# Three FFN-input tile pairs as dense products by token halves, and a LayerNorm end without GpSimd, in a two-layer streaming encoder kernel

## The chip, the cores and the metric

The kernel runs on one core of one Trainium2 chip, as one program of 39,733 instructions. The metric is the device time of one execution in microseconds (us). The engines are TensorE (PE, with its weight loads, PEld), VectorE (DVE), ScalarE (ACT), GpSimd (POOL) and SyncE (SP), which issues most of the DMAs.

## What is computed

Two post-norm layers on a residual stream h of 544 tokens (512 of a prompt and 32 of a sample) and 1024 channels. Each layer runs four token mixers on h, projects their gated sum, and then an FFN with a hidden width of 2816:

```python
    h = layer_norm(ALPHA * h + merged @ w_out, ln1_g, ln1_b)
    a, u = jnp.split(h @ w_ffn_in, 2, axis=-1)
    h = layer_norm(ALPHA * h + (jax.nn.silu(a) * u) @ w_ffn_out, ln2_g, ln2_b)
```

All of it is in float32. The kernel gets that precision from three products of a value's high and low part.

## The kernel before

**Layout.** Channels lie on the 128 partitions, tokens on the free axis, in two halves of 272 tokens (`HB`), called h0 and h1. A value is split into a high part (`hi`, a copy on ACT) and a low part (`lo`, a subtraction on DVE, or on POOL where a letter "g" says so). A product of two such values is three matmuls, hi by hi, lo by hi and hi by lo (`mm3` L712, `product` L737). A dense tile of 128 output channels over 1024 input channels takes 8 x 3 = 24 matmuls for each token half. Its weights are one tile of 128x1024, split as `whi` and `wlo` (`wsplit` L705).

**Order.** The code records every operation, and a planner (`schedule` L544) gives each engine its order, with modelled times; operations inside `ahead` come earlier by a number of places. `places` L179 packs the tiles into the on-chip memory. Where the plan has a gap on PE, `fillers` L626 puts small matmuls into a bank that nobody reads (`bank<-idle`, L648). All other instructions come from one line, L650, so rows are told apart by the tiles' names. Each engine then works its own queue in order.

**From the projection to the FFN.** `project_out` makes eight dense tiles of y = ALPHA*h + merged @ w_out (names `mhl`, `whi`, `wlo`, `y`); the last four for h0 and then for h1, each half followed by `ln_end`, the end of the LayerNorm. That sums over channels on PE with a matrix of ones, makes rs (the inverse deviation) and nmr (minus mean times rs), both named `lnw`, and then runs over eight tiles m: ACT makes t = g*nmr + b, DVE makes y = y*g*rs (`y<-y,gb,lnw`), POOL adds t (`y<-y,lnw`), and y is split into `h0hi`, `h0lo` or `h1hi`, `h1lo`. For h1 ahead of the FFN only odd m are split, since the FFN input needs no others; and after each odd m the differences T1 to T4 of two tiles and both halves are made (`T_plain`, then a split into two parts named `T`), two on DVE and two on POOL ("vvgg").

**FFN input.** `ffn` has 22 pairs of tiles, one of a and one of u, taken in groups of 6, 8 and 8. Each pair is a 2x2 block product in Strassen's form with 7 instead of 8 products of 12 matmuls: 84 where the dense form has 96. The operands on the token side are B11 and B21 (even and odd tiles of h0), B22 (odd tiles of h1) and T1 to T4. On the weight side they are sums of blocks, split as `wop` (128x512; `wsum`, `ws`, `wa`, `wt`, `raw` are what they are made from). B11 and B21 need only h0, so the first `EARLY` = 10 pairs have their two products with them made ahead (`corner` L745, 24 matmuls); half of these have an operand split on POOL (`CORNER`). `strassen` L775 makes the other five. `ln_end` also ends the second LayerNorm of layer 0 ("in").

Of the kernel before, what the change touches and what calls it, by code (L numbers as in the profile page):

```python
# [24 lines left out]
HB = NT // 2  # L25
# [3 lines left out]
FF = 2816  # L29
NM = D // 128  # L30
# [61 lines left out]
LONG = 300  # L92
SELECT = (2, 2, 1)
LEAD = 800
EARLY = 10
PUSH = 120
GROUPS = ((0, 6), (6, 8), (14, 8))
CORNER = ("vg", "vv") * 6
PIECES = ([(0, 512, "v"), (512, 1024, "v")], [(0, 512, "a"), (512, 768, "a"), (768, 1024, "g")], [(0, 1024, "v")])
SPLITS = ("vvvvvvv", "vvvvvvv", "vvvvvvv", "vgvgvgv")  # L100
RESIDUAL = 2
# [45 lines left out]
class Memory:  # L147
# [31 lines left out]
    def places(self, virtual):  # L179
        if self.stage == 1:  # L180
            return self.places_first()
        ops = self.plan.ops
        n, cells = len(self.size), (SBUF - sum(a * b for a, b in RINGS.values())) // self.GRAIN
        size, born, last = (np.array(x) for x in (self.size, self.born, self.last))

        true = virtual.plan.ops
        ready = np.zeros(len(ops))
        for i, op in enumerate(true):
            ready[i] = max((ops[j].done + Plan.HOP[ops[j].eng][op.eng] for j in op.after), default=-1.0)
        for i, op in enumerate(ops):  # L190
            if ready[i] < 0:
                ready[i] = min((ops[j].start for j in true[i].then), default=op.start) - (op.done - op.start) - 1.0
            ready[i] = max(ready[i], min(op.latest, op.start) - MARGIN)
        start, end = np.full(n, 1e9), np.full(n, -1e9)
        for b, users in self.users.items():
            start[b] = min(ready[i] for i in users)
            end[b] = max(ops[i].done for i in users)
        at, done = np.zeros(n, dtype=np.int64), np.zeros(n, dtype=bool)
        life = last - born
        todo = np.flatnonzero(size > 0)  # L200
        self.late = 0.0
        for b in sorted(todo, key=lambda b: (life[b] < 4000, -size[b] * life[b] if life[b] > LONG else b)):
            early = born[b] > last
            late = last[b] < born

            over = np.where(early, end - start[b], np.where(late, end[b] - start, 1e9))
            cost = np.full(cells, -SPARE)
            for x in np.flatnonzero(done & (over > -SPARE)):
                c = cost[at[x]:at[x] + size[x]]
                np.maximum(c, over[x], out=c)  # L210
            top = np.lib.stride_tricks.sliding_window_view(cost, size[b]).max(1)
            k = int(top.argmin())
            if top[k] >= 1e9:
                raise MemoryError((b, size[b], born[b], last[b]))
            at[b], done[b] = k, True
            self.late += max(0, top[k])
        return at
# [438 lines left out]
class Build:  # L656
# [175 lines left out]
            self.split(out(n, 0), out(n, 1), out(n, 1).plain)  # L832

    def hx(self, part, k, h):
        return self.H[h][part][:, k, :]

    def new_h(self, h):
        self.H = list(self.H)
        self.H[h] = [self.mem.tile([128, NM, HB], F32R, name=f"h{h}{n}") for n in ("hi", "lo")]

    def first_load(self, l):
# [922 lines left out]
    def ln_end(self, ln, h, to, scale=1.0):  # L1764
        nc = self.nc
        p1, p2 = self.tps("p1"), self.tps("p2")
        mean, msq, var, rs, nmr = (self.stat(ln, n, h) for n in ("s1", "s2", "var", "rs", "nmr"))
        nc.tensor.matmul(p1[:, :HB], self.ones, mean, start=True, stop=True)
        nc.tensor.matmul(p2[:, :HB], self.ones, msq, start=True, stop=True)
        nc.scalar.activation(mean, p1[:, :HB], AF.Copy, scale=1.0 / D)  # L1770
        nc.scalar.activation(msq, p1[:, :HB], AF.Square, scale=1.0 / D)
        nc.vector.scalar_tensor_tensor(var, p2[:, :HB], 1.0 / D, msq, op0=OP.mult, op1=OP.subtract)
        nc.vector.tensor_scalar(var, var, 0.0, EPS / scale ** 2, op0=OP.max, op1=OP.add)
        nc.scalar.activation(rs, var, AF.Ln)
        nc.scalar.activation(rs, rs, AF.Exp, scale=-0.5)

        nc.vector.scalar_tensor_tensor(var, var, -0.5, rs, op0=OP.mult, op1=OP.mult)
        nc.vector.tensor_tensor(var, var, rs, op=OP.mult)
        nc.vector.scalar_tensor_tensor(rs, var, 1.5, rs, op0=OP.add, op1=OP.mult)
        nc.vector.scalar_tensor_tensor(nmr, mean, -1.0, rs, op0=OP.mult, op1=OP.mult)  # L1780
        gb = ln["gb"]
        y = ln["y"]
        self.new_h(h)
        lt = [self.stat(ln, n, h) for n in ("m0", "var")]
        for m in range(NM):
            yy = y[h][:, m]
            g, b = gb[:, 0, m:m + 1], gb[:, 1, m:m + 1]
            t = lt[m % 2]
            nc.scalar.activation(t, nmr, AF.Identity, scale=g, bias=b)
            nc.vector.scalar_tensor_tensor(yy, yy, g, rs, op0=OP.mult, op1=OP.mult)  # L1790
            nc.gpsimd.tensor_tensor(yy, yy, t, op=OP.add)
            if to != "ffn" or h == 0 or m % 2:
                self.split(self.H[h][0][:, m], self.H[h][1][:, m], yy)
            if to == "ffn" and h and m % 2:
                if m == 1:
                    self.T = [[[self.mem.tile([128, HB], F32R, name="T", twin=p == 1) for _ in range(4)] for p in range(2)]
                              for _ in range(4)]
                self.differences([y[q][:, m - 1 + j] for j in range(2) for q in range(2)],
                                 lambda n, part: self.T[int(n[1]) - 1][part][m // 2], "vvgg")

    def xt(self, block, part, k):

        if block[0] == "T":
            t = self.T[int(block[1]) - 1][part]
            return t[k] if isinstance(t, list) else t[:, k]
        return self.H[int(block[2]) - 1][part][:, 2 * k + int(block[1]) - 1]

    def last_norm(self, l, x, k0, nk, out):

# [78 lines left out]
    def ffn(self, l, out=None):  # L1888
        nc = self.nc
        blocks = ("B11", "B21", "B22", "T1", "T2", "T3", "T4")  # L1890
        w_in, w_out = self.i["w_ffn_in"][l], self.i["w_ffn_out"][l]
        early = []
        for m in range(EARLY):
            pa, t = self.corner(self.load([(w_in[:, m * 128:(m + 1) * 128], 0, 128)], 8), 4, self.xt, CORNER[m])
            g = self.mem.tile([128, HB], F32, name="g")
            with self.nc.ahead(PUSH):
                nc.scalar.activation(g, pa, AF.Silu)
            early.append((g, t))
        for k0, n in GROUPS:
            hid = []  # L1900
            last = k0 + n == NF
            for m in range(k0, k0 + n):
                r = self.blocks(w_in[:, m * 128:(m + 1) * 128], w_in[:, FF + m * 128:FF + (m + 1) * 128], 4)
                g0, t = early[m] if m < EARLY else (self.mem.tile([128, HB], F32, name="g"), None)
                pa, g1, u0, u1 = self.strassen(r, 4, self.xt, t, SPLITS[1])
                if t is None:
                    nc.scalar.activation(g0, pa, AF.Silu)
                nc.scalar.activation(g1, g1, AF.Silu)
                nc.vector.tensor_tensor(u0, g0, u0, op=OP.mult)
                nc.vector.tensor_tensor(u1, g1, u1, op=OP.mult)  # L1910
# [35 lines left out]
        ww = {}  # L1946
# [97 lines left out]
```

## Time and profile before

| | before |
|---|---|
| device time, median of 3 runs | 1996.28 us (1994.49 to 1997.22) |
| profiled execution | 1993.45 us, span of its core 1991.7 us |
| PE busy | 1894.7 us (95%), 14760 matmuls |
| PEld busy | 1809.9 us (91%) |
| DVE busy | 1645.0 us (83%) |
| ACT busy | 1049.4 us (53%) |
| POOL busy | 583.7 us (29%) |
| mean granted clock of TensorE | 0.987 |

The profile is of one execution; its times count from the span's start. Layer 0 takes up to about 1045 us: mixers and projection to 597, the LayerNorm and the FFN input's start from there to 657, the FFN to 960, its last group and the second LayerNorm to 1045. Layer 1 repeats this, with its LayerNorm and FFN start at 1579 to 1640 us. The busy share of an engine is a mean over all of that; a row of a stage or of the timeline tells what one stretch waits for. Idle matmuls count as busy.

### The profile page before, as it was taken

How to read it: one execution, taken by the hardware profiler on the slowest of the kernel's cores; microseconds unless marked ns; L12 is line 12 of the kernel's file. 1: busy time of each engine (PE TensorE's matmuls, PEld its weight loads, DVE VectorE, ACT ScalarE, POOL GpSimd, SP SyncE). 2: the span in 40 equal slices, each digit the busy share in tenths (PEclk: the TensorE clock that was granted, in tenths of full speed). 3: DMA queues.
4: the chain of work that ended last, by engine and by line, in shares of the span. 5: the costliest groups of instructions: out<-in, count | busy, mean ns of one | idle time of the engine just before them, and what ended most of it. 6: DMA issues, size and time to landing. Idle time of an engine off the chain costs nothing.

```text
span 1991.7 us, 39733 instructions
## 1 busy us (share of the span) xinstructions
PE 1894.7 (95%) x14760; PEld 1809.9 (91%) x14760; DVE 1645.0 (83%) x3539; ACT 1049.4 (53%) x2190; POOL 583.7 (29%) x586
## 2 busy tenths in 40 slices
PE   9999999999998999999989999999999889999997
PEld 8988788999997999999889878899999888999996
DVE  5898768787879999988779876787978799998875
ACT  4465434555637555555455654355555465555552
POOL 1424040134345221221423341302343542213101
PEclk9999999999999999999989999999999999999998
DMA  8322133666624788777403222356665157977741
GB/s 223 86 76 61 51 94 90 145 156 147 156 86 127 163 190 192 171 180 174 124 19 90 68 85 52 91 116 147 150 147 156 42 148 175 229 170 169 172 122 46
DMA packets 406530, 253.34 MB, mean 127 GB/s; under 512 B 27432, under 2 KB 381144, under 8 KB 406080
## 3 DMA queue, kind: packets, MB, share of 16 engines
q1 hardware_dynamic: 379264, 202.56, 36.9%
q0 software_dynamic: 27072, 48.25, 14.5%
q8 instruction: 116, 1.90, 0.4%
q14 instruction: 78, 0.64, 0.1%
HBM read 192.47 MB, written 7.82 MB: 101 GB/s over the span
## 4 chain that ended last, share of the span: by engine, by line
PE 63%; DVE 22%; DMA 7%; issue 3%; ACT 3%; POOL 2%; SPq 1%; POOLq 0%; ACTq 0%; DVEq 0%
PE bank L650 62%; DVE wop L650 5%; DMA ws<-wa 3%; DVE y L650 3%; DVE wsum L650 1%; DVE lnw L650 1%; DVE st L650 1%; DVE q L650 1%; DVE wlo L650 1%; SPq L650 1%; DVE score L650 1%; ACT wop L650 1%; DVE su L650 1%; PE bank L648 1%; DVE sv L650 1%
## 5 line engine op out<-in xcount | busy, mean ns | idle before, releaser
L650 PE MATMUL bank<-T,wop 128*128 128x272 f32 x3744 | 504.7, 291 | 19.2 <-DVE su L650 8.4
L650 PEld LDWEIGHTS bank<-T,wop 128*128 128x128 f32 x3744 | 484.4, 190 | 23.4 <-DVE su L650 10.8
L650 PE MATMUL bank<-h0hi,wop 128*128 128x272 f32 x1248 | 264.6, 294 | 3.5 <-ACT st L650 2.7
L650 PEld LDWEIGHTS bank<-h0hi,wop 128*128 128x128 f32 x1248 | 206.5, 191 | 9.3 <-ACT st L650 4.8
L650 POOL DMA_DIRECT2D ws<-wa x94 | 81.7, 869 | 398.8 <-DVE wop L650 115.8
L650 PE MATMUL bank<-h0lo,wop 128*128 128x272 f32 x624 | 181.7, 291 | 6.9 <-DVE h0lo L650 6.7
L650 POOL DMA_DIRECT2D wt<-raw x94 | 83.1, 889 | 333.1 <-DVE wop L650 64.8
L650 DVE TENSOR_TENSOR wop<-raw,wop 128x512 fp32r<-128x512 f32 (+1 forms) x178 | 135.4, 765 | 38.1 <-ACT wop L650 37.9
L650 ACT ACTIVATE wop<-raw 128x512 fp32r<-128x512 f32 (+1 forms) x188 | 115.5, 619 | 90.5 <-PE bank L650 82.3
L650 ACT ACTIVATE wop<-wsum 128x512 fp32r<-128x512 f32 (+1 forms) x188 | 116.7, 620 | 86.6 <-PE bank L650 48.5
L650 PE MATMUL bank<-q,wop 128*128 128x272 f32 x1176 | 153.2, 290 | 4.5 <-DVE q L650 2.0
L650 PEld LDWEIGHTS bank<-q,wop 128*128 128x128 f32 x1176 | 148.9, 188 | 7.7 <-DVE q L650 3.1
L650 DVE TENSOR_TENSOR wop<-wsum,wop 128x512 fp32r<-128x512 f32 (+1 forms) x188 | 131.7, 701 | 13.8 <-ACT wop L650 12.8
L650 DVE TENSOR_TENSOR wlo<-raw,whi 128x1024 fp32r<-128x1024 f32 (+1 forms) x80 | 107.9, 1355 | 29.6 <-PE bank L650 14.5
L650 PE MATMUL bank<-h1hi,wop 128*128 128x272 f32 x624 | 131.4, 289 | 0.0
L650 PEld LDWEIGHTS bank<-h0lo,wop 128*128 128x128 f32 x624 | 119.1, 191 | 8.1 <-DVE h0lo L650 8.1
L650 ACT ACTIVATE whi<-raw 128x1024 fp32r<-128x1024 f32 (+1 forms) x80 | 83.5, 1048 | 74.1 <-PE bank L650 43.5
L650 PE MATMUL bank<-h1hi,whi 128*128 128x272 f32 (+1 forms) x384 | 115.9, 302 | 1.8 <-ACT h1hi L650 1.8
L650 PE MATMUL bank<-h0hi,whi 128*128 128x272 f32 (+1 forms) x384 | 116.7, 304 | 0.0
L650 PE MATMUL bank<-h1lo,whi 128*128 128x272 f32 (+1 forms) x384 | 112.0, 292 | 3.1 <-DVE h1lo L650 3.1
L650 PE MATMUL bank<-h0lo,whi 128*128 128x272 f32 (+1 forms) x384 | 111.5, 290 | 2.6 <-DVE h0lo L650 2.6
L650 PE MATMUL bank<-h1hi,wlo 128*128 128x272 f32 (+1 forms) x384 | 112.1, 292 | 0.0
(459 smaller groups left out, 5096.8 us busy)
## 6 DMA issues: line engine op xcount, KB each, us to landing
raw<-in_w_in_dram SPq DMA_DIRECT2D x46, 512.0 KB, 3.7
raw<-in_w_ffn_in_dram SPq DMA_DIRECT2D x88, 256.0 KB, 3.8
ws<-wa POOLq DMA_DIRECT2D x86, 256.0 KB, 4.5
wt<-raw POOLq DMA_DIRECT2D x86, 256.0 KB, 4.2
raw<-in_w_in_dram SPq DMA_DIRECT2D x68, 256.0 KB, 3.5
wa<-in_w_ffn_in_dram SPq DMA_DIRECT2D x44, 256.0 KB, 3.3
ws<-in_w_ffn_in_dram SPq DMA_DIRECT2D x44, 256.0 KB, 2.9
wt<-in_w_ffn_in_dram SPq DMA_DIRECT2D x44, 256.0 KB, 4.4
```

The costliest lines, as they stand in the source:

```text
L648: self.real.tensor.matmul(out, x, x, start=False, stop=True, skip_group_check=True)
L650: call(*a, **k)
```

## The change

1. In `ffn` the first three pairs (`DENSE` = 3) are made in dense form: their six weight tiles are split and kept, the products with h0 are made for all six tiles, then those with h1, and silu and the product of a and u go half by half.
2. `EARLY` goes from 10 to 6, and pairs below `DENSE` have no corner: three corners (pairs 3 to 5) remain, with both operands split on DVE.
3. `ln_end` makes y*rs and adds nmr on DVE, and ACT applies g and b (the result is y). All eight tiles of h1 are split, into four tiles of memory (`apart`) rather than two. The differences are all made on DVE ("vvvv").
4. `places` tries four values of `LONG` where memory doesn't fit.

```diff
-EARLY = 10
+DENSE = 3
+EARLY = 6
-CORNER = ("vg", "vv") * 6
+CORNER = ("vv",) * 12
...
         for m in range(NM):
             yy = y[h][:, m]
             g, b = gb[:, 0, m:m + 1], gb[:, 1, m:m + 1]
             t = lt[m % 2]
-            nc.scalar.activation(t, nmr, AF.Identity, scale=g, bias=b)
-            nc.vector.scalar_tensor_tensor(yy, yy, g, rs, op0=OP.mult, op1=OP.mult)
-            nc.gpsimd.tensor_tensor(yy, yy, t, op=OP.add)
-            if to != "ffn" or h == 0 or m % 2:
-                self.split(self.H[h][0][:, m], self.H[h][1][:, m], yy)
+            nc.vector.tensor_tensor(t, yy, rs, op=OP.mult)
+            nc.vector.tensor_tensor(t, t, nmr, op=OP.add)
+            nc.scalar.activation(yy, t, AF.Identity, scale=g, bias=b)
+            self.split(self.hx(0, m, h), self.hx(1, m, h), yy)
...
-                                 lambda n, part: self.T[int(n[1]) - 1][part][m // 2], "vvgg")
+                                 lambda n, part: self.T[int(n[1]) - 1][part][m // 2], "vvvv")
...
+        first = [[] for _ in range(DENSE)]
+        ww = []
+        for h in range(2):
+            for m in range(DENSE):
+                if not h:
+                    ww.append([self.wsplit(self.load([(w_in[:, c:c + 128], 0, 128)], 8), 0, 128, 8, None)
+                               for c in (m * 128, FF + m * 128)])
+                g = self.mem.tile([128, HB], F32, name="g")
+                u = self.mem.tile([128, HB], F32, name="su")
+                pa, pu = self.bank("f"), self.bank("f")
+                for ps, w in zip((pa, pu), ww[m]):
+                    self.mm3(ps, w, 128, 8, self.hx, h)
+                nc.scalar.activation(g, pa[:, :HB], AF.Silu)
+                nc.vector.tensor_tensor(u, g, pu[:, :HB], op=OP.mult)
+                first[m].append(u)
+        early = {}
+        for m in range(DENSE, EARLY):
...
-                r = self.blocks(w_in[:, m * 128:(m + 1) * 128], w_in[:, FF + m * 128:FF + (m + 1) * 128], 4)
...
+                if m < DENSE:
+                    u0, u1 = first[m]
+                else:
+                    r = self.blocks(w_in[:, m * 128:(m + 1) * 128], w_in[:, FF + m * 128:FF + (m + 1) * 128], 4)
```

**The order on PE in layer 0, after the last product of the first half.** Before, the last corner (wop_974) is followed by products with T; afterwards the sixth dense tile (whi_945, wlo_946) is followed by products with h1. Before:

```order
L650 MATMUL bank_63<-h0hi_874,wop_974 128x272 x2
L650 MATMUL bank_63<-h0lo_875,wop_974 128x272
L650 MATMUL bank_63<-h0hi_874,wop_974 128x272
L650 MATMUL bank_62<-T_878,wop_983 128x272
L650 MATMUL bank_62<-T_882,wop_983 128x272
```

And now:

```order
L661 MATMUL bank_62<-h0hi_874,whi_945 128x272
L661 MATMUL bank_62<-h0lo_875,whi_945 128x272
L661 MATMUL bank_62<-h0hi_874,wlo_946 128x272
L661 MATMUL bank_65<-h1hi_876,whi_929 128x272
L661 MATMUL bank_65<-h1lo_878,whi_929 128x272
L661 MATMUL bank_65<-h1hi_876,wlo_930 128x272
```

The h1 products of the dense pairs and the three corners now stand between the first half and the first T product.

**The order on DVE in layer 0, from the last two steps on rs and nmr (the first two rows) of the first half.** Before:

```order
L650 SCALAR_TENSOR_TENSOR lnw_842<-lnw_840,lnw_842 128x272
L650 SCALAR_TENSOR_TENSOR lnw_844<-lnw_834,lnw_842 128x272
L650 SCALAR_TENSOR_TENSOR y_751<-y_751,gb_848,lnw_842 128x272 x6
L650 TENSOR_TENSOR h0lo_875<-y_751,h0hi_874 128x272
L650 SCALAR_TENSOR_TENSOR y_751<-y_751,gb_848,lnw_842 128x272
L650 TENSOR_TENSOR h0lo_875<-y_751,h0hi_874 128x272
```

And now:

```order
L661 SCALAR_TENSOR_TENSOR lnw_842<-lnw_840,lnw_842 128x272
L661 SCALAR_TENSOR_TENSOR lnw_844<-lnw_834,lnw_842 128x272
L661 TENSOR_TENSOR wlo_938<-raw_936,whi_937 128x1024
L661 TENSOR_TENSOR lnw_838<-y_751,lnw_842 128x272
L661 TENSOR_TENSOR wlo_941<-raw_939,whi_940 128x1024
L661 TENSOR_TENSOR lnw_838<-lnw_838,lnw_844 128x272
L661 TENSOR_TENSOR lnw_840<-y_751,lnw_842 128x272
L661 TENSOR_TENSOR wlo_946<-raw_944,whi_945 128x1024
L661 TENSOR_TENSOR h0lo_875<-y_751,h0hi_874 128x272
```

Three weight splits of the dense tiles stand among the first tiles' steps, and the first h0lo comes after three steps of 272 columns instead of six.

**The order on ACT at the same place.** The first two rows are the sums' results, `lnw_842` is rs. Before:

```order
L650 ACTIVATE lnw_834<-bank_66 128x272
L650 ACTIVATE lnw_836<-bank_66 128x272
L650 ACT_TABLE_LOAD
L650 ACTIVATE lnw_842<-lnw_840 128x272
L650 ACTIVATE lnw_846<-y_751 128x272
L650 ACTIVATE lnw_842<-lnw_842 128x272
```

And now:

```order
L661 ACTIVATE lnw_834<-bank_66 128x272
L661 ACTIVATE lnw_836<-bank_66 128x272
L661 ACTIVATE whi_937<-raw_936 128x1024
L661 ACTIVATE whi_945<-raw_944 128x1024
L661 ACTIVATE lnw_846<-y_751 128x272
L661 ACT_TABLE_LOAD
L661 ACTIVATE lnw_842<-lnw_840 128x272
L661 ACTIVATE lnw_842<-lnw_842 128x272
L661 ACTIVATE lnw_847<-y_751 128x272
L661 ACTIVATE whi_940<-raw_939 128x1024
L661 ACTIVATE whi_948<-raw_947 128x1024
L661 ACTIVATE y_751<-lnw_838,gb_848 128x272
```

Four weight copies now stand ahead of the first y, two of them ahead of the steps that make rs.

Over the whole program the order has 13,855 matmuls that are not idle ones before and 13,927 now, and 415 and 202 idle matmuls.

## Rows read from the trace of the kernel before

**Rows 1.** The page, part 1: busy us (share of the span) and instructions.

```profile
PE 1894.7 (95%) x14760; PEld 1809.9 (91%) x14760; DVE 1645.0 (83%) x3539; ACT 1049.4 (53%) x2190; POOL 583.7 (29%) x586
```

**Rows 2.** Windows: length, busy of PE, PEld, DVE, ACT, POOL, clock, DMA share, GB/s.

```profile
655.00:960.00 305.00, 296.54 (x2348) 294.03 (x2347) 274.59 (x568) 171.58 (x347) 67.23 (x75) 0.99 0.77 184
960.00:1045.00 85.00, 74.89 (x546) 71.02 (x545) 66.54 (x139) 42.53 (x97) 30.92 (x38) 0.94 0.18 48
```

**Rows 3.** Windows, the FFN input's start in layer 0, and shorter stretches.

```profile
597.10:656.50 59.40, 50.11 (x400) 46.80 (x398) 55.13 (x87) 39.14 (x91) 30.77 (x32) 0.91 0.44 112
740.00:750.00 10.00, 10.00 (x82) 10.00 (x81) 9.75 (x20) 4.83 (x11) 2.62 (x3) 1.00 1.04 227
600.00:610.00 10.00, 8.94 (x53) 7.48 (x54) 8.79 (x16) 5.65 (x16) 5.99 (x7) 0.83 0.00 0
640.00:650.00 10.00, 5.42 (x55) 4.92 (x53) 9.35 (x12) 4.02 (x9) 7.69 (x9) 0.73 0.44 92
```

**Rows 4.** Windows, PE's instructions with wop alone: length, busy, clock, DMA.

```profile
597.10:656.50 59.40, 42.15 (x289) 0.91 0.44 112
```

**Rows 5.** Waits of PE from 575 to 660 us: total us, times, longest.

```profile
PE bank L650 <- DVE h0lo L650: 3.0, 2, 2.6
```

**Rows 6.** Timeline of PE, both layers: start, us, instruction, count, idle before and its releaser.

```profile
597.14 0.28 PE L650 MATMUL bank<-h0hi,wop 128*128 128x272 f32 x1
...
637.11 2.41 PE L650 MATMUL bank<-T,wop 128*128 128x272 f32 x18
...
646.35 0.82 PE L650 MATMUL bank<-T,wop 128*128 128x272 f32 x2 [2.83 <-DVE T L650]
...
656.50 0.29 PE L650 MATMUL bank<-h1hi,wop 128*128 128x272 f32 x1
...
1578.99 0.29 PE L650 MATMUL bank<-h0hi,wop 128*128 128x272 f32 x1
...
1639.63 0.29 PE L650 MATMUL bank<-h1hi,wop 128*128 128x272 f32 x1
```

**Rows 7.** Timeline of DVE, LayerNorm 1 of layer 0.

```profile
594.42 4.66 DVE L650 SCALAR_TENSOR_TENSOR y<-y,gb,lnw 128x272 f32<-128x272 f32 x6
599.00 0.99 DVE L650 TENSOR_TENSOR h0lo<-y,h0hi 128x272 fp32r<-128x272 f32 x1
...
603.17 0.43 DVE L650 TENSOR_TENSOR y<-y,lnw 128x272 f32<-128x272 f32 x1
603.53 0.43 DVE L650 TENSOR_TENSOR h0lo<-y,h0hi 128x272 fp32r<-128x272 f32 x1
...
652.80 0.90 DVE L650 TENSOR_TENSOR T<-T_plain,T 128x272 fp32r<-128x272 f32 x2 [0.65 <-POOL T_plain L650]
...
654.58 0.69 DVE L650 TENSOR_TENSOR wop<-ws,wop 128x512 fp32r<-128x512 f32 x1
655.18 0.69 DVE L650 TENSOR_TENSOR wop<-wsum,wop 128x512 fp32r<-128x512 f32 x1
```

**Rows 8.** Timeline of POOL at the same place.

```profile
595.23 5.40 POOL L650 TENSOR_TENSOR y<-y,lnw 128x272 f32<-128x272 f32 x6 [1.03 <-ACT lnw L650]
```

**Rows 9.** Groups of DVE by shape: count, busy us, mean ns, idle before and releasers.

```profile
L650 DVE TENSOR_TENSOR wlo<-raw,whi 128x1024 fp32r<-128x1024 f32 x78 | 106.4, 1371 | 29.6 <-PE bank L650 14.5 <-ACT whi L650 10.1 <-DMA raw<-in_w_out_dram 3.0
```

**Rows 10.** Timeline of ACT at the LayerNorm of rows 7.

```profile
596.37 0.60 ACT L650 ACTIVATE lnw<-lnw,gb 128x272 f32<-128x272 f32 x1
596.97 0.43 ACT L650 ACTIVATE h0hi<-y 128x272 fp32r<-128x272 f32 x1
```

**Rows 11.** Timelines of DVE and PE at LayerNorm 2 of layer 0.

```profile
989.12 3.18 DVE L650 SCALAR_TENSOR_TENSOR y<-y,gb,lnw 128x272 f32<-128x272 f32 x5
992.22 1.78 DVE L650 TENSOR_TENSOR wlo<-raw,whi 128x1024 fp32r<-128x1024 f32 x1
993.92 0.99 DVE L650 TENSOR_TENSOR h0lo<-y,h0hi 128x272 fp32r<-128x272 f32 x1
...
994.96 0.39 PE L650 MATMUL bank<-h0lo,whi 128*128 128x272 f32 x1 [2.57 <-DVE h0lo L650]
```

More of the change, by code (lines that the diff above doesn't have):

```diff
@@ L197, in places, with fit @@
             end[b] = max(ops[i].done for i in users)
+        for long in (LONG, LONG / 2, LONG * 2, LONG / 4):
+            try:
+                return self.fit(start, end, cells, long)
+            except MemoryError as e:
+                error = e
+        raise error
+    def fit(self, start, end, cells, long):
+        size, born, last = (np.array(x) for x in (self.size, self.born, self.last))
+        n = len(size)
         at, done = np.zeros(n, dtype=np.int64), np.zeros(n, dtype=bool)
@@ L201, in places @@
         self.late = 0.0
-        for b in sorted(todo, key=lambda b: (life[b] < 4000, -size[b] * life[b] if life[b] > LONG else b)):
+        for b in sorted(todo, key=lambda b: (life[b] < 4000, -size[b] * life[b] if life[b] > long else b)):
             early = born[b] > last
@@ L834, in hx, with new_h @@
     def hx(self, part, k, h):
-        return self.H[h][part][:, k, :]
-    def new_h(self, h):
+        v = self.H[h][part]
+        return v[k] if isinstance(v, list) else v[:, k, :]
+    def new_h(self, h, apart=False):
         self.H = list(self.H)
+        if apart:
+            t = [[self.mem.tile([128, NM // 2, HB], F32R, name=f"h{h}{n}") for _ in range(2)] for n in ("hi", "lo")]
+            self.H[h] = [[p[m % 2][:, m // 2] for m in range(NM)] for p in t]
+            return
         self.H[h] = [self.mem.tile([128, NM, HB], F32R, name=f"h{h}{n}") for n in ("hi", "lo")]
@@ L1782, in ln_end @@
         y = ln["y"]
-        self.new_h(h)
+        self.new_h(h, to == "ffn" and h)
         lt = [self.stat(ln, n, h) for n in ("m0", "var")]
@@ L1805, in xt @@
             return t[k] if isinstance(t, list) else t[:, k]
-        return self.H[int(block[2]) - 1][part][:, 2 * k + int(block[1]) - 1]
+        return self.hx(part, 2 * k + int(block[1]) - 1, int(block[2]) - 1)
     def last_norm(self, l, x, k0, nk, out):
@@ L1891, in ffn @@
         w_in, w_out = self.i["w_ffn_in"][l], self.i["w_ffn_out"][l]
-        early = []
-        for m in range(EARLY):
+        first = [[] for _ in range(DENSE)]
[15 more added lines that the diff above has]
+        for m in range(DENSE, EARLY):
             pa, t = self.corner(self.load([(w_in[:, m * 128:(m + 1) * 128], 0, 128)], 8), 4, self.xt, CORNER[m])
@@ L1897, in ffn @@
                 nc.scalar.activation(g, pa, AF.Silu)
-            early.append((g, t))
+            early[m] = g, t
         for k0, n in GROUPS:
@@ L1902, in ffn @@
             for m in range(k0, k0 + n):
-                r = self.blocks(w_in[:, m * 128:(m + 1) * 128], w_in[:, FF + m * 128:FF + (m + 1) * 128], 4)
[L1904 to L1910, printed above, removed]
+                if m < DENSE:
+                    u0, u1 = first[m]
+                else:
+                    r = self.blocks(w_in[:, m * 128:(m + 1) * 128], w_in[:, FF + m * 128:FF + (m + 1) * 128], 4)
+                    g0, t = early[m] if m < EARLY else (self.mem.tile([128, HB], F32, name="g"), None)
+                    pa, g1, u0, u1 = self.strassen(r, 4, self.xt, t, SPLITS[1])
+                    if t is None:
+                        nc.scalar.activation(g0, pa, AF.Silu)
+                    nc.scalar.activation(g1, g1, AF.Silu)
+                    nc.vector.tensor_tensor(u0, g0, u0, op=OP.mult)
+                    nc.vector.tensor_tensor(u1, g1, u1, op=OP.mult)
                 if last:
```

## The prediction, made before the changed kernel was timed

> **What bounds the kernel now.** I read the page's first part, the busy times by stage, the waits of TensorE (PE), and then the timelines of PE, VectorE (DVE) and GpSimd (POOL) in the stages with a gap. PE is busy for 1894.7 of 1991.7 us [rows 1]: 97 us are idle, and they are not spread evenly. The FFN and the later projections run nearly closed: a steady stretch of 10.00 us holds 82 matmuls, 0.122 us each [rows 3], and 655 to 960 us has PE busy for 296.54 of 305.00 [rows 2]. So where PE is fed, time is matmuls times 0.122 us, and DVE at 83% of the span only matters where PE waits for it.
>
> The gap that the change aims at is the end of the first LayerNorm (LN1) and the start of the FFN input. In layer 0 this goes from the first h0 product at 597.14 to the first h1 product at 656.50 [rows 6], 59.36 us. The program's order puts 288 products there, 240 corner products (10 corners of 24) and 48 with T operands; the windows count 289 with the one that starts at the edge [rows 4]. Fed, they take 288 x 0.122 = 35.1 us, so 59.36 - 35.1 = **24.2 us are lost in layer 0**. Layer 1 goes from 1578.99 to 1639.63 [rows 6], 60.64 us for the same 288: **25.5 us lost**. PE's busy time hides most of this (50.11 of 59.40, [rows 3]), since of its 400 matmuls there [rows 3] only 289 are products [rows 4] and nearly all others idle ones in the gaps, and the granted clock is 0.91 there, 0.73 in 640 to 650 us, against 1.00 in the steady stretch [rows 3]: the real products are stretched too. The named waits are only the longest single ones: 3.0 us for h0lo at the start [rows 5], 2.83 us for T [rows 6].
>
> Why PE starves is seen on DVE. The two products' operands are made in an order that needs the LayerNorm of both halves before the differences T. Beside POOL's additions DVE's scale step takes 4.66/6 = 0.78 us, and an h0lo 0.99; with POOL quiet the same tile size goes at a pitch of 0.36 us (603.17 to 603.53) [rows 7]. POOL takes 5.40/6 = 0.90 us for each addition and so sets the pace of a step that needs three engines [rows 8]. At the end of the stretch the last T differences wait for POOL's T_plain until 652.80 [rows 7]. Nothing else is left for PE then: the first T product at 637.11 has only 18 matmuls ready, and the next come at 646.35 [rows 6].
>
> **The change, part by part.**
>
> *Three dense pairs, extra work.* A dense pair is 2 tiles x 2 halves x 24 = 96 products, a Strassen pair 84. Three pairs in two layers: 3 x 12 x 2 = 72 products more, 72 x 0.122 = **+8.8 us**, 4.4 in each layer, all on PE's own path, with no cover.
>
> *The order at LN1.* What PE can do before it needs a T was 240 products; now it is 3 x 96 = 288 dense ones, half of them on h0 and half on h1, and 72 of three corners: 360, or 43.9 us. The order of PE in the section on the change shows h1 products where T products stood. The h1 products need only the LayerNorm of h1, which comes ahead of the differences. So the question is when DVE has the first Strassen operands and T. From the last nmr (594.4, where the first scale starts, [rows 7]) the new order of DVE has 128 instructions up to the first Strassen operand: 111 of 272 columns, 13 weight sums of 512 columns and 4 wlo of 1024. With POOL out of the way: 111 x 0.36 = 40.0; 13 x 0.60 (pitch of wop at 654.58 and 655.18, [rows 7]) = 7.8; 4 x 1.37 (mean of wlo, [rows 9]) = 5.5. Together 53.3 us, so 647.7. DVE also waits for ScalarE (ACT) twice for each tile; ACT needs 0.93 us for a tile (0.60 and 0.43, one after the other from 596.37, [rows 10]) against DVE's 3 x 0.36 = 1.08, so ACT keeps up, but the first of each half and a silu or two do not hide: I take 3 us, an estimate from the 3.0 us of h0lo waits of before [rows 5]. T products then start at 651. PE began at 597.1 and has 43.9 us of work: 651 - 597.1 - 43.9 = **10 us lost in layer 0** in place of 24.2. In layer 1 the sixth dense weight's wlo stands behind nmr of h1 in DVE's order, and 33 idle matmuls stand ahead of its tile on PE; I add 2 us: **12 lost** in place of 25.5. Gains: 24.2 - 10 - 4.4 = 9.8 and 25.5 - 12 - 4.4 = 9.1, together **-18.9**. Bounds of the loss: 6.7 us for each layer if the 3 us of waits vanish, and 24 if DVE's order keeps T back until 665; break-even is the loss of before less 4.4, so 19.8 and 21.1.
>
> Queued behind the three wlo that now stand among DVE's first tiles are the h0lo of all tiles; PE waits for those. Their price is 3 x 1.37 = 4.1 us, but the six contended steps of before cost 4.66 to the first h0lo, and three instructions now do with 1.1: first h0lo stays near 599, so I cost this at nothing; without that relief it would be 4 us in each layer (part of the bounds).
>
> *LayerNorm 2.* The same three-step end runs at LN2 of layer 0, where PE is busy for 74.89 of 85.00 us [rows 2]. There h0lo comes 4.80 us after the first scale (989.12 to 993.92) and PE waits 2.57 us for it [rows 11]; h1 runs the same steps. Two steps of 0.36, two on ACT (0.93) and the difference make about 2.9 us with hand-overs, so some 1.7 us earlier for each half, 3.4 for both, and the tiles behind follow at 3 x 0.36. Bounds 0 (a wlo of 1.78 us also stands there) and 5; I take **-4**.
>
> *Rest of the FFN input.* Three pairs less in Strassen form relieve DVE in the first group: a pair costs it 7 operands and 2 sums of 0.60 and 7 small ones of 0.36, 7.9 us, a dense pair 2 x 1.37 + 2 x 0.36 = 3.5. PE loses 305.00 - 296.54 = 8.5 us there [rows 2], so little of it can come back; bounds -6 and +3 (three pairs' weights are held in SBUF meanwhile); I take **-2**. POOL's corner operands go to DVE: counted in the 13. The differences that went to POOL: counted in the 111. The planner's small reordering of the mixers: 0, bounds +-4.
>
> **A rule weighed.** The trace has PE's weight loads at 91% and DVE at 83%, against POOL's 29% [rows 1]. The Trainium skill ("Perfetto Trace Analysis", section Identifying the Most-Contended Engine) says to find the engine of highest occupancy, for TensorE by its LDWEIGHTS busy share, and to improve that first. The change adds work to the two busiest engines and takes it from the idlest, so by that rule the sum would be the extra products alone, +8.8, and the time 2005. The trace speaks against it in this stretch: weight loads are busy there for 46.80 of 59.40 us, those of the idle matmuls among them [rows 3].
>
> The sum: -18.9 - 4 - 2 = -25 us. The profiled execution took 1993.45 us (span 1991.7 and 1.75 around it) and lies 2.8 below the median 1996.28 of the runs; taken from the median, 1996.3 - 25 = **1971**.
>
> **Rivals.** *Half of it.* DVE and ACT work in order, and weight splits now stand among the LayerNorm steps. If a wlo has to wait for its whi, and whi for a weight tile that has not landed or for memory that PE has not released, all pieces behind it are late. For: ACT's order (shown with the change) has four whi ahead of the first y, two of them even ahead of the two steps that make rs. Against: before, wlo stood among these steps too at LN2 (992.22) and cost its own 1.78 us only [rows 11]. Loss 17 and 18 instead of 10 and 12: gains 2.8 and 3.1, with LN2 -4: **1986**.
>
> *More.* The waits for ACT do not show, loss 6.7 in each layer: gains 13.1 and 14.4; LN2 -5, FFN input -6: 1996.3 - 38.5, **1958**. For: POOL's contention disappears from the whole stretch. Against: DVE's 53 us stay ahead of PE's 44.
>
> *Slower.* The stalls stay. DVE takes over from POOL 8 additions' work in each half and half the splits of the differences, and its queue becomes the end of everything: if T is late by 14 us more than I think, at 665, the loss is the old 24 to 25, LN2 shows nothing, and the 72 products remain: 1996.3 + 8.8 = **2005**. It decides from T at 597.1 + 43.9 + 20 = 661. For: T's last one is at 652.80 now with POOL's help. Against: the sum of DVE's instructions, 647.7.
>
> *No effect.* Planner and memory give back what is won, for instance by later weight loads: **1996**. The DMA engines move nothing in 600 to 610 us [rows 3], so the dense tiles' weights find room; little speaks for it.
>
> **How the numbers follow.** The forecast 0.61, half of it 0.15, more 0.12, slower 0.08, no effect 0.04. About 0.2%, 4 us, is what a measurement of this kernel can tell from no change. Faster: 0.61 + 0.12 + nearly all of 0.15, 0.87; same: 0.04 and the edge of the half case, 0.05; slower 0.08. The forecast's own bounds (loss +-4 in each layer, LN2, rest) reach from 1960 to 1983; to hold 8 in 10 the range takes in the half case and most of the larger gain: 1956 to 1988.
>
> **What would show it.** Right: in the new trace the stretch from the first h0 product to the first T product has 360 products in some 54 us, the clock stays near 1.00, T products follow each other without waits of 2 us and more, DVE's 272-column steps stand at 0.36 us from 594 on, and POOL is quiet. Wrong: waits for h0lo or h1lo of more than 4 us (half), or T after 661 (slower). The 72 products should show as PE's count of real matmuls.

## The result, and the profile after

| | before | after |
|---|---|---|
| device time, median | 1995.38 us, 4 runs (1989.07 to 1997.22) | **1947.57 us**, 4 runs (1941.77 to 1948.34) |
| ratio to before | | 0.976, 95% interval 0.9731 to 0.9788 |
| profiled execution, span | 1993.45, 1991.7 us | 1947.43, 1945.7 us |

The change saves 47.8 us, about twice the 25 us that were forecast. The direction was right, the size was not, and 1947.6 lies below the range's lower end of 1956.

The page of the changed kernel, part 1 (answers to [rows 1]):

```profile
PE 1881.4 (97%) x14619; PEld 1801.8 (93%) x14619; DVE 1601.7 (82%) x3549; ACT 1043.9 (54%) x2160; POOL 499.8 (26%) x500
```

The busy shares have hardly moved, and PE is busy for 13 us less although it makes 72 products more. The windows of the changed kernel say more. Columns as in [rows 2]; the first two lines go from the first h0 product to the first T product in layer 0 and layer 1, the third is the FFN input behind the first product with a hidden value (`bank<-q,wop`) in layer 0, and the last a steady piece of the first stretch:

```profile
591.15:641.32 50.17, 47.94 (x353) 46.44 (x354) 47.57 (x122) 34.61 (x81) 4.54 (x4) 0.97 0.29 76
1555.66:1606.20 50.54, 48.89 (x397) 48.05 (x398) 49.51 (x122) 39.38 (x86) 4.84 (x6) 1.00 0.33 88
664.40:914.65 250.25, 246.53 (x1957) 244.44 (x1956) 221.85 (x464) 144.28 (x298) 53.64 (x61) 1.00 0.74 176
620.00:630.00 10.00, 10.00 (x82) 10.00 (x81) 10.00 (x29) 6.38 (x16) 0.86 (x1) 1.00 0.16 29
```

In [rows 3] the same place had stretches at a clock of 0.73 with PE half empty; now the clock is 0.97 and 1.00 on the mean, and 620 to 630 us runs at the steady 82 matmuls in 10 us. Not all of the stretch is closed: in layer 0 the first h0 product starts at 591.18, 2.4 us behind the last w_out product, and the granted clock of 590 to 595 us is 0.72, with products 0.23 us apart in place of 0.125. POOL is down to 4.54 us of 50.

The three longest of PE's waits from 585 to 645 us (answers to [rows 5]), and PE's timeline where T begins (answers to [rows 6]):

```profile
PE bank L661 <- ACT h0hi L661: 1.4, 1, 1.4
PE bank L661 <- DVE su L661: 0.7, 1, 0.7
PE bank L661 <- ACT h1hi L661: 0.5, 1, 0.5
```

```profile
641.22 0.29 PE L661 MATMUL bank<-h0hi,wop 128*128 128x272 f32 x1
641.34 1.66 PE L661 MATMUL bank<-T,wop 128*128 128x272 f32 x12
...
644.36 1.93 PE L661 MATMUL bank<-T,wop 128*128 128x272 f32 x14
```

No wait for T is left, and no idle matmuls stand between the T products. DVE's timeline in that stretch (answers to [rows 7]):

```profile
588.10 0.44 DVE L661 TENSOR_TENSOR lnw<-y,lnw 128x272 f32<-128x272 f32 x1
588.45 1.22 DVE L661 TENSOR_TENSOR wlo<-raw,whi 128x1024 fp32r<-128x1024 f32 x1
...
591.42 0.43 DVE L661 TENSOR_TENSOR h0lo<-y,h0hi 128x272 fp32r<-128x272 f32 x1
591.77 0.43 DVE L661 TENSOR_TENSOR lnw<-lnw,lnw 128x272 f32<-128x272 f32 x1
...
629.80 1.48 DVE L661 TENSOR_TENSOR T<-T_plain,T 128x272 fp32r<-128x272 f32 x4
...
637.81 0.69 DVE L661 TENSOR_TENSOR wop<-wsum,wop 128x512 fp32r<-128x512 f32 x1 [0.42 <-ACT wop L661]
...
639.18 0.69 DVE L661 TENSOR_TENSOR wop<-ws,wop 128x512 fp32r<-128x512 f32 x1
```

Steps of 272 columns follow each other at 0.35 us, the last four T splits take 1.48 us together where the last two ended at 653.7 before, and the weight split takes 1.22 us. The last T is there at 631.3. A T product also needs a weight operand, though, and in the program's order the first one reads the `wop<-ws,wop` of the last row, which is there at 639.87. PE comes to it at 641.34, 1.5 us later: PE is the later of the two, but only just.

**Where the time went.** For every kernel below I take the time lost in a stage as its length in the trace, less its number of matmuls that are not idle ones times 0.122 us (0.1222 unrounded, the pitch of the steady stretch in [rows 3]). The stages are cut at PE's milestones: the last product with w_out, the first with a hidden value, the last of the FFN input. "LN1" goes from the last w_out product to the first `q,wop`, "FFN" from there to the end of the FFN input, "LN2" is the first 45 us behind the last product of layer 0. The first number of a pair is layer 0, the second layer 1.

| us lost | mixers | LN1 | FFN | LN2 |
|---|---|---|---|---|
| before | 56.1, 39.6 | 25.0, 26.6 | 19.3, 18.9 | 17.4 |
| after | 49.1, 45.1 | 10.6, 8.0 | 12.6, 12.4 | 14.3 |
| change | -7.0, +5.5 | -14.4, -18.6 | -6.7, -6.5 | -3.1 |

The LN1 stretches give 33.0 us less lost for 8.8 us of added products, 24.2 net. The FFN input behind gives 13.2, LN2 3.1, the mixers 1.5 net, w_out's products 2.2 and the layers' last products 0.7. Together 44.9 of the 46.0 us between the two spans.

### The profile page after: what moved, and what is told of

The parts are those of the page before. It is cut to its first block, busy times and chain, and to the rows that moved or that the text cites. A ratio compares the mean times of both kernels' runs of the same rounds, so it can differ in the third digit from the quotient of the medians.

```text
span 1945.7 us, 39164 instructions
## 1 busy us (share of the span) xinstructions
PE 1881.4 (97%) x14619; PEld 1801.8 (93%) x14619; DVE 1601.7 (82%) x3549; ACT 1043.9 (54%) x2160; POOL 499.8 (26%) x500
## 3 DMA queue, kind: packets, MB, share of 16 engines
q0 software_dynamic: 25344, 45.10, 13.7%
## 4 chain that ended last, share of the span: by engine, by line
PE 35%; DVE 7%; DMA 3%; ACT 2%; issue 2%; POOL 1%; SPq 0%; POOLq 0%; ACTq 0%; DVEq 0%
PE bank L661 35%; DMA ws<-wa 1%; DVE wop L661 1%; DVE lnw L661 1%; DVE wlo L661 1%; DVE y L661 1%; DMA raw<-in_w_ffn_out_dram 0%; DVE st L661 0%; DVE wsum L661 0%; DVE score L661 0%; DVE q L661 0%; DMA xs<-rk 0%; DVE sv L661 0%; ACT whi L661 0%; POOL lnw L661 0%
## 5 line engine op out<-in xcount | busy, mean ns | idle before, releaser
L661 PE MATMUL bank<-T,wop 128*128 128x272 f32 x3456 | 461.3, 289 | 5.5 <-DVE su L661 4.3
L661 PEld LDWEIGHTS bank<-T,wop 128*128 128x128 f32 x3456 | 444.5, 189 | 7.4 <-DVE su L661 5.1
L661 PE MATMUL bank<-h0hi,wop 128*128 128x272 f32 x1152 | 243.9, 291 | 0.5 <-DVE acc L661 0.4
L661 PEld LDWEIGHTS bank<-h0hi,wop 128*128 128x128 f32 x1152 | 189.7, 188 | 3.5 <-DVE acc L661 0.6
L661 PE MATMUL bank<-h0hi,whi 128*128 128x272 f32 (+1 forms) x480 | 147.7, 308 | 3.3 <-ACT h0hi L661 3.3
L661 ACT ACTIVATE wop<-wsum 128x512 fp32r<-128x512 f32 (+1 forms) x176 | 109.0, 620 | 71.7 <-PE bank L661 45.1
L661 DVE TENSOR_TENSOR wlo<-raw,whi 128x1024 fp32r<-128x1024 f32 (+1 forms) x92 | 122.9, 1344 | 29.4 <-PE bank L661 13.4
L661 PE MATMUL bank<-h1hi,whi 128*128 128x272 f32 x480 | 143.8, 300 | 1.2 <-DVE su L661 0.7
L661 PE MATMUL bank<-h0lo,whi 128*128 128x272 f32 (+1 forms) x480 | 140.9, 294 | 1.8 <-DVE h0lo L661 1.8
L661 PE MATMUL bank<-h0hi,wlo 128*128 128x272 f32 (+1 forms) x480 | 141.0, 294 | 1.2 <-DVE wlo L661 1.1
L661 PE MATMUL bank<-h1lo,whi 128*128 128x272 f32 x480 | 139.3, 290 | 0.1
L661 PE MATMUL bank<-h1hi,wlo 128*128 128x272 f32 x480 | 139.3, 290 | 0.0
```

Of the source, the lines that this page charges most:

```text
L661: call(*a, **k)
```

## Experiments

Each time is the median of a run beside the kernel before (1993.3 to 1993.6 us there).

### Each half of the change alone

`ln_only`: no dense pair and the ten corners of before.

```diff
-DENSE = 3
-EARLY = 6
+DENSE = 0
+EARLY = 10
-CORNER = ("vv",) * 12
+CORNER = ("vg", "vv") * 6
...
-        self.new_h(h, to == "ffn" and h)
+        self.new_h(h, DENSE and to == "ffn" and h)
...
-            self.split(self.hx(0, m, h), self.hx(1, m, h), yy)
+            if to != "ffn" or h == 0 or m % 2:
+                self.split(self.hx(0, m, h), self.hx(1, m, h), yy)
```

> The new LayerNorm end and the differences on VectorE alone, with no dense pair, ten corners and half of their operands on GpSimd as before. Theory (the two parts share the gain: the LayerNorm part shortens the wait for T, the dense part fills it and relieves the later FFN): PE has 240 products, 29 us, and T comes about 10 us earlier than before, so some 10 of 24 us are saved in each layer, and about 4.6 us at LayerNorm 2: 1995 - 24 = 1971, range 1965 to 1978, with the 20 us lost later in each FFN input unchanged. Rival (GpSimd's contention was nearly all of it): over 35 us gained, 1960 or less.

Measured: 1996.38 us, ratio 1.0015 (1.0000 to 1.0030). Neither expectation: no gain at all. The stages tell why. LN1 loses 17.3 and 21.5 us in place of 25.0 and 26.6, LN2 14.7 in place of 17.4, so some 15 us are won there. But the mixers of layer 0 lose 70.5 us in place of 56.1, with the same 3954 matmuls in another order, and those of layer 1 44.1 in place of 39.6: 18.9 us are given back in stages that the edit does not touch.

`dense_only`: the dense pairs, six for `EARLY`, but the old LayerNorm end and GpSimd's share of the differences and of the corners' operands.

```diff
-            nc.vector.tensor_tensor(t, yy, rs, op=OP.mult)
-            nc.vector.tensor_tensor(t, t, nmr, op=OP.add)
-            nc.scalar.activation(yy, t, AF.Identity, scale=g, bias=b)
+            nc.scalar.activation(t, nmr, AF.Identity, scale=g, bias=b)
+            nc.vector.scalar_tensor_tensor(yy, yy, g, rs, op0=OP.mult, op1=OP.mult)
+            nc.gpsimd.tensor_tensor(yy, yy, t, op=OP.add)
...
-                                 lambda n, part: self.T[int(n[1]) - 1][part][m // 2], "vvvv")
+                                 lambda n, part: self.T[int(n[1]) - 1][part][m // 2], "vvgg")
-CORNER = ("vv",) * 12
+CORNER = ("vg", "vv") * 6
```

> Three dense pairs and six-pair corners, but the old LayerNorm end with GpSimd's additions and two of the four differences on GpSimd, and GpSimd's half of the corner operands. Theory: T comes no earlier than before and even h1 tiles are split too, so the wait at LayerNorm 1 falls only by the 120 more products that stand there (14.6 us) less their own 4.4, some 8 us in each layer, and the later FFN input loses 6 us less in each layer: 1995 - 28 = 1967, range 1960 to 1978. Rival (the LayerNorm part is nearly all): 1985 or more.

Measured: 1964.09 us, ratio 0.9844 (0.9821 to 0.9867). As the theory has it, at 1967. LN1 loses 19.8 and 17.3 us, FFN 12.6 and 12.0. Summed over LN1 and FFN of both layers the losses are 89.8 before, 75.8 for the LayerNorm part, 61.7 for the dense part and 43.6 for both: 14.0 and 28.1 alone, 46.2 together (the 8.8 us of added products are not taken off the last two). Neither is the whole.

### Parts of the LayerNorm end

`oldend`: the changed kernel with the three lines of the old end (the first six lines of the diff above); `vvgg`: the changed kernel with "vvgg" alone.

> The changed kernel with the old LayerNorm end (ScalarE's t, VectorE's scale, GpSimd's addition); the differences all on VectorE and no operand split on GpSimd, as changed. Theory (it is the addition on GpSimd, beside which VectorE runs at half speed, that makes h0lo and h1lo late): the stretch up to the first T loses 17 us in each layer in place of 9.5 and 7.0, and LayerNorm 2 loses 4 us more: 1948 + 20 = 1968, range 1958 to 1975. Rival (it is the differences): up to 2 us in each layer, 1946 to 1954.

Measured: 1958.32 us, ratio 0.9822 (0.9801 to 0.9842), on the theory's side, at the lower edge of its range, since the mixers happen to lose 7.2 us less than in the changed kernel. LN1 loses 16.7 and 13.5 us in place of 10.6 and 8.0, FFN 16.0 and 15.2, LN2 17.4 as before the change. DVE's groups from 580 to 650 us in this kernel (count, busy us, mean ns):

```profile
L661 DVE SCALAR_TENSOR_TENSOR y<-y,gb,lnw 128x272 f32<-128x272 f32 x16 | 10.4, 687 | 0.0
L661 DVE TENSOR_TENSOR wlo<-raw,whi 128x1024 fp32r<-128x1024 f32 x4 | 6.6, 1640 | 0.0
```

The same view of the changed kernel, 588 to 650 us:

```profile
L661 DVE TENSOR_TENSOR lnw<-lnw,lnw 128x272 f32<-128x272 f32 x17 | 7.1, 428 | 0.0
L661 DVE TENSOR_TENSOR lnw<-y,lnw 128x272 f32<-128x272 f32 x16 | 6.7, 429 | 0.0
L661 DVE TENSOR_TENSOR wlo<-raw,whi 128x1024 fp32r<-128x1024 f32 x4 | 4.9, 1215 | 0.0
```

The means hide two lengths, as a piece of DVE's timeline in `oldend` shows, at the start of POOL's first additions (582.40):

```profile
581.60 0.90 DVE L661 SCALAR_TENSOR_TENSOR y<-y,gb,lnw 128x272 f32<-128x272 f32 x2
582.42 1.21 DVE L661 TENSOR_TENSOR wlo<-raw,whi 128x1024 fp32r<-128x1024 f32 x1
583.56 1.00 DVE L661 SCALAR_TENSOR_TENSOR y<-y,gb,lnw 128x272 f32<-128x272 f32 x1
```

Of the 16 scale steps ten take 0.49 us and six 1.00 to 1.04; of the four weight splits one takes 1.21 us, as in the changed kernel, and three 1.78. So a step either keeps its length or is 0.5 to 0.6 us longer here, about as much for 272 columns as for 1024: that looks like one wait and not like a slower engine. Over the whole kernel 19 of the 48 scale steps are long, and none of the 18 that have no POOL instruction beside them. Two DVE steps without POOL (0.43 us each, overlapping to a pitch of 0.35) cost about as much as the mean of one beside it. The Trainium skill ("SBUF — State Buffer", section Who interferes with whom) says that a DVE instruction with two inputs in SBUF contends with a GpSimd instruction that reads SBUF, and calls the shared ports an exclusive lock. The rows agree as far as they go (steps of 1.00 us beside steps of 0.49); no run here has POOL's addition alone, so whether the two strictly take turns stays open.

> The changed kernel with two of the four differences on GpSimd, as before. Theory (the wait ahead of T is closed by products in any case, and GpSimd's four times two differences of about 1 us only slow VectorE beside them): 1 to 3 us more lost ahead of T in each layer: 1948 to 1955. Rival (VectorE is the bound of the stretch and eight operations less help it): 1940 to 1945.

Measured: 1963.29 us, ratio 0.9851 (0.9826 to 0.9875): above both. The stretches alone agree with the theory (LN1 11.6 and 13.3 us, FFN 11.6 and 13.0, some 6 us more in all); 10 of the 16 us are lost in the mixers of layer 0 (59.1 in place of 49.1). What "vvgg" itself costs is the 6 us, of which 2 to 4 are within what two profiles of one program differ by.

### Corners and dense pairs

> The changed kernel with seven corners (pairs 3 to 9) ahead in place of three. Theory A (the later FFN input lost 20 us before because corners drawn ahead leave pairs of 60 products, 7.3 us of PE, against 6.7 us and more of VectorE): the waits at the end of the first group and in the second, some 3 and 4 us in each layer, come back, while the gap ahead of T is already closed: 1948 + 10 = 1958, range 1952 to 1964. Theory B (it was the three Strassen pairs less, VectorE's work of 13 us): the later FFN input stays as it is, 1944 to 1949.

```diff
-EARLY = 6
+EARLY = 10
```

Measured: 1945.45 us, ratio 0.9754 (0.9727 to 0.9780), as theory B in the time. In the stages it is mixed: FFN loses 13.3 us in layer 0 and 17.8 in layer 1 (12.6 and 12.4 with three corners), which is theory A's loss in one layer; the mixers of layer 1, with 37.1 in place of 45.1 us, hide it in the time.

> The kernel before with six corners in place of ten, nothing else. Both theories: 96 products less stand ahead of T, so 11.7 us more are lost in each layer at LayerNorm 1. Theory A (corners drawn ahead starve the later pairs): the later FFN input gives back 5 to 6 us in each layer: 1995 + 12 = 2007. Theory B: nothing given back, 2018.

Measured: 2101.14 us, ratio 1.053 (1.0512 to 1.0549): nobody's number. The mixers lose 108.7 and 86.4 us, with 1124 idle matmuls in the order in place of 415, while FFN loses 13.5 and 12.1. In this kernel the packing of memory fails in the planner's second draft, and the first, rough one is issued. The changed kernel tries four values of `LONG` there, so the next two runs ask for that part.

```diff
-        for long in (LONG, LONG / 2, LONG * 2, LONG / 4):
+        for long in (LONG,):
```

> The changed kernel with one value of LONG in the packing of memory, as before the change; all else as changed. Theory (the packing decides the plan of the whole program, and the new tiles do not fit with LONG = 300 in the second draft, so the first draft's rough plan is kept): both mixer stages get some 50 us longer, as in the kernel with six corners and nothing else, 1948 + 100 = 2048, range 2020 to 2080; PE loses there, in the first LayerNorm's stretch at most 3 us more. Rival (the trial of four values is only a safeguard): 1944 to 1951.

Measured: 1943.38 us, ratio 0.9750 (0.9724 to 0.9777). The theory falls. The order of instructions is the same as in the changed kernel, row for row: the draft that it takes packs with LONG = 300, and the trial only serves a later draft that isn't used. So this is a second measurement of one program: 1947.57 and 1943.38 us, 0.2% apart, and by its profile LN1 loses 9.9 and 10.9 us, FFN 11.2 and 13.6, mixers 51.1 and 45.8. Two profiles of one program differ by up to 3 us in a stage.

> The kernel before with six corners and the trial of four values of LONG, nothing else. Theory A (fewer corners relieve the later FFN input, and the 106 us of the run with six corners alone were the rough plan): mixers within 8 us of before, from the first product with a hidden value to the end of the FFN input 13 us lost in each layer in place of 19, 6 us more lost ahead of it: 1990 to 2000. Rival (six corners cost the time themselves): over 2060.

```diff
-EARLY = 10
+EARLY = 6
...
+        for long in (LONG, LONG / 2, LONG * 2, LONG / 4):
+            try:
+                return self.fit(start, end, cells, long)
...
```

Measured: 2003.85 us, ratio 1.0051 (1.0032 to 1.0069). This is 4 us above theory A's range and far below the rival's 2060: the rough plan made up 97 of the 108 us between the run with six corners alone and the kernel before. With six corners LN1 loses 31.8 and 30.4 us, FFN 14.4 and 17.8: theory A's 13 us behind T came out, nearly, in layer 0 alone.

> The new LayerNorm end and differences, no dense pair, six corners with half of their operands on GpSimd. Against the run with ten corners it tells what corners alone do to the FFN input behind T. Theory (a pair whose corner was made ahead has 60 products against nearly the VectorE work of a whole pair, so VectorE falls behind in the second group): behind the first hidden-value product 13 us are lost in each layer in place of 18.5, ahead of it some 5 more. Rival (it was the three Strassen pairs less): 18 us there. In time 1985 to 2005, since the mixers differ from plan to plan.

```diff
-DENSE = 3
+DENSE = 0
-CORNER = ("vv",) * 12
+CORNER = ("vg", "vv") * 6
```

(and the two other edits of `ln_only`). Measured: 1984.87 us, ratio 0.9958 (0.9944 to 0.9972). FFN loses 13.1 and 14.2 us with six corners, 18.9 and 18.1 with ten (`ln_only`); LN1 loses 22.6 and 23.2 against 17.3 and 21.5. The theory holds: corners alone, with no dense pair, move some 5 us in each layer. The FFN window of layer 0, first with ten corners (`ln_only`):

```profile
701.10:945.80 244.70, 237.73 (x1879) 235.00 (x1878) 219.73 (x464) 136.12 (x282) 52.89 (x61) 0.99 0.76 181
```

and with six (`ln_early6`):

```profile
675.60:927.90 252.30, 248.57 (x1972) 246.10 (x1971) 227.24 (x474) 145.60 (x300) 52.77 (x59) 1.00 0.74 177
```

The longer window holds 93 matmuls more. Idle ones are 29 of the first and 12 of the second, so it has 110 products more, 13.4 us, in 7.6 us more, and PE's idle time falls from 7.0 to 3.7 us.

> The changed kernel with no corner at all, 72 products less ahead of T. Theory (T comes when VectorE is done, whatever PE has to do; the corners' operands cost VectorE 12 x 0.6 = 7 us in each layer, so T comes up to 7 us earlier): the 8.8 us of products missing ahead of T are partly made up, 2 to 5 us more lost in each layer: 1955, range 1945 to 1965, apart from the mixers. Rival (the stretch is bound by PE alone): no more lost, 1948.

```diff
-EARLY = 6
+EARLY = 3
```

Measured: 1941.36 us, ratio 0.9741 (0.9717 to 0.9764), on the rival's side and below it. LN1 loses 14.4 and 9.1 us (10.6 and 8.0, or 9.9 and 10.9, with three corners), FFN 9.6 and 11.4. What is lost ahead of T comes back behind it. With dense pairs in place the corners are worth nothing that can be measured; this kernel, simpler by three corners, is as fast as the changed one.

> Two dense pairs and four corners. Products ahead of T: 192 + 96 = 288 in place of 360, PE has 35.2 us of work in place of 43.9, and 24 products fewer in the whole program (-2.9 us). Theory: T is set by VectorE, which saves two weight splits of 1.37 us, so 5 to 6 us more are lost in each layer ahead of T: 1948 + 11 - 3 = 1956, range 1948 to 1968. Rival (the third dense pair only adds work): 1944.

```diff
-DENSE = 3
+DENSE = 2
```

Measured: 1965.66 us, ratio 0.9870 (0.9846 to 0.9894). LN1 loses 15.2 and 12.2 us, some 4 us more in each layer where the theory has 5 to 6; 9 of the 18 us are lost in the mixers of layer 0 again (58.4).

### The same operations in another order

`draft3` takes the planner's third draft.

```diff
-            if best is None or mem.plan.end < best[0]:
+            if _ < 3:
```

> The changed kernel issued in the order of the planner's third draft in place of the one that it takes itself; the operations are the same. Theory (the order of the mixers is a matter of chance within 10 us and has no part in what was changed): the LayerNorm and FFN input stretch loses 20 to 26 us in each layer as in the changed kernel (23 and 21), the mixers differ by up to 15 us in either direction: 1940 to 1965. Rival (the 6.5 us won in the mixers of layer 0 belong to the change): mixers of layer 0 stay at 549 us, 1944 to 1950.

Measured: 1974.98 us, ratio 0.9897 (0.9870 to 0.9924): 27 us slower than the changed kernel with the same operations, and beyond the range. Mixers lose 55.0 and 55.5 us in place of 49.1 and 45.1, and LN1 of layer 1 18.3 in place of 8.0. The two longest of PE's waits from 1555 to 1680 us show a part of what stands in the way there:

```profile
PE bank L661 <- POOL lnw L661: 2.4, 1, 2.4
PE bank L661 <- DVE wlo L661: 2.0, 1, 2.0
```

The theory is right in kind: the 7.0 us that the mixers of layer 0 gave are a matter of the plan. Over the plans run here (all but the rough one) the mixers of layer 0 lose 44.3 to 70.5 us, those of layer 1 37.1 to 55.5, with nothing changed in them.

## Why the prediction was too small

**LN1, the main step: right, and a little short.** The sum of DVE's instructions was to end at 647.7, and T to start at 651, 53.9 us behind the last w_out product; it started 52.5 us behind it (588.8 to 641.34). The losses forecast were 10 and 12 us. Measured are 10.6 and 8.0, in the second profile of the same program 9.9 and 10.9. DVE's sum holds, its few waits included: 52.9 us from the last nmr (586.96) to the operand of the first T product (639.87), where 53.3 were forecast. PE comes 1.5 us later, and from 620 us on without a gap, so of the 3 us set down for waits on ACT little is seen at this point. The delay of the first h0lo, costed at nothing, shows at the start instead: the first h0 product comes 2.4 us behind the last w_out product in layer 0 and 0.9 in layer 1, against 0.1 before. The 2 us added for layer 1 did not come. The net gain of 24.2 us (22.0 by the second profile) stands against 18.9 forecast.

**The extra products: right.** 72 at the steady pitch; in layer 0 all but one corner's 12 of the 360 products stand ahead of the first T product, and 620 to 630 us, full at that pitch, shows them on PE's path.

**The rest of the FFN input: this step failed.** I took its gain as 2 us, since PE was idle there for only 305.00 - 296.54 = 8.5 us [rows 2]. It gave 13.2. The idle time was the wrong measure. Counting products, as I had done for LN1 one paragraph earlier, the kernel before loses 19.3 and 18.9 us in that stage. Its window:

```profile
693.15:939.80 246.65, 238.59 (x1886) 236.29 (x1885) 223.46 (x469) 137.75 (x287) 53.78 (x61) 0.99 0.76 182
```

Of the 1886 matmuls 23 are idle ones; 1863 x 0.122 = 227.3 us of 246.65, while the busy time is 238.59. In that busy time 2.35 us are idle matmuls, and from 778 to 798 us the products are slower, at a granted clock of 0.91. Of the 21 us by which the forecast fell short of the 46.0 between the spans, this step makes 11.2, LN1 5.3, w_out's products 2.2 and the mixers 1.5. A second thing was left out of that step: what the corners do behind T. I counted `EARLY` only as filling ahead of T. A pair whose corner was made ahead has 60 products left, 7.3 us, against five operands and two sums of 0.60 and seven steps of 0.35, 6.7 us, on DVE, whose queue also has the hidden values to split. In that part of the kernel before DVE has no slack, and the first group's end waits for it:

```profile
PE bank L650 <- DVE su L650: 3.8, 3, 2.7
PE bank L648 <- DVE su L650: 2.8, 1, 2.8
```

```profile
690.00:710.00 20.00, 15.88 (x122) 14.53 (x121) 19.48 (x50) 11.19 (x28) 3.44 (x4) 1.00 0.63 144
718.00:738.00 20.00, 20.00 (x161) 20.00 (x161) 19.89 (x48) 9.90 (x21) 4.26 (x5) 1.00 0.99 226
```

The first two rows are PE's longest waits from 658 to 960 us (L648 is an idle matmul; the wait of 2.7 us ends at 696.74); in the changed kernel the longest from 641 to 930 us is 1.8 us.

A corner is thus a loan. It fills PE ahead of T and is paid back behind it; ten corners against six move about 5 us in each layer (`ln_only` and `ln_early6`), and the sum over both stages hardly changes (75.8 and 73.1 us). The dense pairs fill the same gap without the loan: they take work from DVE for good (7.9 us against 3.5 for a pair, by the prediction's count). The runs with three dense pairs lose 15.6, 12.5 and 10.5 us in FFN, as a mean of the layers, with seven, three and no corners. The direction is shown: in all four pairs of kernels that differ in their corners (before to `early6_fit`, `ln_only` to `ln_early6`, `early10` to the changed one, that to `early3`) both layers lose less in FFN with fewer corners, by 0.7 to 5.8 us. The size is not fixed: layers of one pair differ by up to 4.7 us, and `oldend`, with the changed kernel's corners and dense pairs, loses 16.0 and 15.2. The three Strassen pairs less show no gain of their own that can be told from this: `ln_early6` to the changed kernel, 13.7 to 12.5 as a mean of the layers, with three corners less besides. That the corners are the larger part of the 13.2 us is thus the reading that fits best, and not measured by itself.

**LN2: right.** -4 forecast, -3.1 measured (5.1 in the second profile). Over the kernels whose LayerNorm 2 has the new end it loses 12.3 to 16.2 us, over those with the old one 16.3 to 18.0, without the rough plan.

**The planner: bounded far too closely.** I gave its reordering +-4 us. For this change the mixers came out at -7.0 and +5.5, nearly nothing in sum, so it is not why the forecast missed. But that the sum stayed within +-4 was luck: the same operations in another draft took 27 us more.

**The rivals.** "More" (1958) had the right mechanism, POOL's contention gone and T no longer late, and its price was too low by the same FFN step. "Half of it" needed waits of whi on memory or DMA. They exist, on ACT's timeline of the changed kernel, for memory that PE releases, but PE waits only 1.4 us for h0hi after them:

```profile
586.38 1.06 ACT L661 ACTIVATE whi<-raw 128x1024 fp32r<-128x1024 f32 x1 [1.50 <-PE bank L661]
588.26 1.06 ACT L661 ACTIVATE whi<-raw 128x1024 fp32r<-128x1024 f32 x1 [0.81 <-PE bank L661]
590.05 0.61 ACT L661 ACTIVATE y<-lnw,gb 128x272 f32<-128x272 f32 x1 [0.73 <-DVE lnw L661]
```

"Slower" put T at 665, or 657 on this kernel's clock, which began 8.3 us earlier; T started at 641. The rule of the Trainium skill that was weighed ("Perfetto Trace Analysis", Identifying the Most-Contended Engine) would have had 2005; the trace is against it: weight loads went from 91% to 93% of a span that is 46.0 us shorter, and the added products went where PE had nothing to do.

**What stays open.** Why one order of the mixers loses 44 us and another 70 was not followed to single waits. And between the two medians of one program, 1947.57 and 1943.38, and early3's 1941.36 no order of merit can be given.

## What to carry to other kernels

Count useful work in every stage, not only in the one that the change aims at: stage length less products times the steady pitch found 19 us where busy time showed 8. Work that is drawn ahead to fill a gap is a loan if its share on the follower engine stays behind; making the work in a form that costs the busy engine more but leaves no such share can pay: LN1 and FFN of both layers lose 44.5 us with three dense pairs and no corner (`early3`), beside 8.8 us of added products, and 73.1 with six corners and no dense pair (`ln_early6`). And where a planner orders the whole program, judge an edit by the stages that it touches, from the trace: here the total moved by up to 27 us for the order alone, and half of a change looked worth nothing (`ln_only`) that saved some 15 us where it acts.

## What was not expected of the hardware

VectorE's steps of 272 columns kept a pitch of 0.35 us from 588 to 631 us with GpSimd quiet, while beside the LayerNorm's additions on GpSimd a scale step of that size took either 0.49 or some 1.0 us and a weight split of 1024 columns either 1.21 or 1.78, 0.5 to 0.6 us more for the short step and for the long one. One program, measured in two sets of runs, came out 0.2% apart, and single stages of it by up to 3 us.
